# Attention of a hybrid block: six slots for a pair of heads instead of eight, and splits cut into a high and a low step

## The chip, the cores and the metric

The kernel runs on one core of a Trainium2 chip. The core has a matrix engine (PE), two element-wise engines (DVE, the vector engine, and ACT, the scalar engine, which alone computes exponentials), POOL (here: additions of a mask, and the issue of stores) and SP, which issues loads. Each engine takes its instructions in the order of its own queue and waits at the head of it for semaphores. The metric is the device time of one execution in microseconds.

## The reference

One layer of a streaming encoder on 1024 positions of width 1024. All of it is float32. The part that the change touches is the forgetting attention and the first half of the branch projection, which is computed beside it.

```python
def forgetting_attention(q, k, v, logf):
    c = jnp.cumsum(logf, axis=1).transpose(0, 2, 1)
    for s0 in range(0, s_len, Q_BLOCK):                   # query tiles of 128
        logits = einsum("bqhd,bkhd->bhqk", q[:, s0:s1], k[:, :s1]) * scale
        logits = logits + c[:, :, s0:s1, None] - c[:, :, None, :s1]
        logits = jnp.where(kpos <= qpos, logits, -jnp.inf)
        p = jax.nn.softmax(logits, axis=-1)
        outs.append(einsum("bhqk,bkhd->bqhd", p, v[:, :s1]))

ya = g_b * causal_depthwise_conv(g_c * hc, conv_w)
ya_d = jnp.einsum("bsc,cd->bsd", ya, w_branch[0])         # branch A, 512 -> 1024
yb_d = jnp.einsum("bsc,cd->bsd", yb, w_branch[1])         # branch B, of the attention
merged = jax.nn.sigmoid(gate_conv) * ya_d + jax.nn.sigmoid(gate_attn) * yb_d
```

There are 8 heads of 64 columns. Ahead of this stand the pre-norm and the input projection, behind it the output projection, two norms and a SwiGLU feed-forward layer.

## The kernel before

**Precision.** A float32 product is made of three passes over operands that are split in two: `hi`, a rounded copy that ACT writes, and `lo`, the remainder, a subtraction on DVE that needs `hi`. Each such split is thus one ACT instruction and one DVE instruction behind it (`split`, and for the queries and keys `split_q` and `split_k`).

**Pairs, rows, slots.** Heads are taken two at a time: pairs j = 0 to 3. The query tile i of a pair (a *row*, i = 0 to 7) needs keys up to its own tile, so it has i + 1 key blocks of 128. The list `steps` names a row for each slot: rows 7 down to 0 for pairs 0 to 2, and rows 3, 2, 1, 0, 7, 6, 5, 4 for pair 3; 32 slots in all. The work of a row passes through four stages, spread over three slots:

- slot t: PE writes the scores `sp` (three passes, both heads e = 0, 1 side by side in the array). A row of over 512 keys takes both of the two `S` buffers, one a head; a shorter row takes one buffer for both heads. DVE adds the bias `cb` and finds the row maximum in one instruction (`row_max`, writes `pt` and `nm`; in the queue listings below the two rows `ISA pt,nm<-sp,cb` and `ISA nm`). ACT takes the exponential in place (`expo`).
- slot t + 1: PE transposes `pt` by blocks into `tps`, at most 4 blocks to a bank, two banks (`turn_bank`). Each bank is drained to `ptT` by ACT or DVE. The drains are called `da`, `db` (head 0, blocks 0 to 3 and 4 to 7) and `dc`, `dd` (head 1).
- slot t + 2: PE multiplies `ptT` with the values into `po` (`pv_pair`). Behind a row with i a multiple of 4 ACT copies four finished rows to `yb`.

POOL adds the causal mask to the diagonal columns of `cb` just ahead of each row (`mask_of`).

**Fill.** Between the transposes of head 0 and those of head 1 PE does units of branch A (`pba`): one unit is three matmuls of 512 columns, four units make one output tile of 128 columns and half the positions, after which DVE multiplies it by a gate (`um`). 13 of the 16 tiles lie in the slots, 52 units; the table `units` says how many in which slot, from slot 8 on. The other three tiles follow after the last slot, and then branch B (`pbb`).

**The order is written out by hand.** From the last gate job to the end of the slots every instruction keeps its place in the program; nothing is moved by a scheduler. The table `at` lists what is appended to the end of a slot: loads (`load_pair`, `load_ya`, `load_wa`, `load_sg`, `load_wb`), splits (`split_q`, `split_k`, `split_ya`, `split_wa`, `split_wb`), the reciprocals of the row sums (`inverse`) and the divisions (`divide`). In a slot DVE sees: row maximum of head 0, `db`, row maximum of head 1, its share of `dc` and `dd`, the `um` products, and then the list of `at`. The slots 2 to 33 are the loop

```python
for t in range(2, NU + 2):
    ...
    for m in muls:
        m()
    for f in at.pop(t, ()):
        f()
```

Slots 0 and 1 (rows 7 and 6 of pair 0) are written into `last_pair`, between the products of the last gate job.

## Time and profile before

| | us |
|---|---|
| time, median of 3 runs | 1373.96 (1373.7 to 1374.09) |
| the profiled execution's own time | 1373.6 |
| its span on the core | 1371.8 |
| slots 2 to 33 and the three tiles behind them, first `sp` of slot 2 to first `pbb` | 422.26 to 582.48, 160.22 |
| pair 0's slots from 2 on / pair 1's eight / pair 2's eight / pair 3's eight, by their first `sp` | 21.88 / 43.44 / 40.25 / 37.39 |
| the rest, slots 32 and 33 and the three tiles | 17.26 |

Rows of the timeline read: start, duration, engine, line, operation, output and inputs, shape, count of like instructions merged into the row, and in brackets the idle time before it and what ended it. Almost every instruction has line 73, since a helper records them all, so tiles tell them apart. Matmuls are pipelined and their ends are modelled: a duration on PE overlaps the next instruction's, so what a piece of PE work costs is read from its start to the start of the next piece. Transposes and the products with the values work on plain float32; a value product counts as two matmul records.

### The profile page before, as it was taken

What the parts mean: (1) busy time and instruction counts of PE and PEld (TensorE: products, weight loads), DVE (VectorE), ACT (ScalarE), POOL (GpSimd) and SP (SyncE); (2) the same over time, 40 slices, a digit from 0 to 9 for tenths busy, and PEclk for the clock granted to TensorE, in tenths of its full rate; (3) what the DMA queues carried; (4) which work ended last, traced back from release to release, by engine and by line L of the source; (5) the groups of instructions that cost most, each with busy time, mean ns of one, the idle gap of its engine ahead of it and who ended that gap; (6) DMA issues with size and microseconds to landing.
All of it is one profiled execution on the core that took longest, in us unless ns stands there. A gap on an engine that the chain in (4) does not pass through costs nothing.

```text
span 1371.8 us, 17726 instructions
## 1 busy us (share of the span) xinstructions
PE 1341.8 (98%) x6725; PEld 1096.7 (80%) x6725; DVE 933.8 (68%) x1449; ACT 536.1 (39%) x853; POOL 127.9 (9%) x256
## 2 busy tenths in 40 slices
PE   7999999999999999999999999999999999999997
PEld 7978888888877777788887788888888888888886
DVE  6874767755446665685669698776677666676585
ACT  6641322233346654633447332232223223444452
POOL 0101000011112111000001112100111011000000
PEclk9999999999999999999999999999999999999999
DMA  6332423343315444462234565323333235975541
GB/s 216 97 111 85 137 57 99 94 123 100 114 71 185 135 131 152 139 215 85 77 124 153 158 201 179 100 73 110 108 107 105 95 115 205 352 251 197 168 162 62
DMA packets 153398, 186.88 MB, mean 136 GB/s; under 512 B 9424, under 2 KB 106768, under 8 KB 153312
## 3 DMA queue, kind: packets, MB, share of 16 engines
q1 hardware_dynamic: 138576, 137.19, 32.2%
q0 software_dynamic: 14736, 48.54, 9.7%
q8 instruction: 53, 0.87, 0.3%
q14 instruction: 33, 0.27, 0.1%
HBM read 136.62 MB, written 49.09 MB: 135 GB/s over the span
## 4 chain that ended last, share of the span: by engine, by line
PE 86%; DVE 5%; ACT 3%; DMA 3%; issue 2%; POOL 0%; DVEq 0%; ACTq 0%; POOLq 0%
PE b L73 52%; PE pd L73 15%; PE pm L73 5%; PE pbb L73 3%; PE pba L73 3%; PE po L73 2%; PE tps L73 2%; PE sp L73 2%; DVE t L73 1%; ACT pt L73 1%; DVE pt L73 1%; PE pv L73 1%; PE ma L73 1%; DMA pre_dram<-s 1%; PE tp L73 1%
## 5 line engine op out<-in xcount | busy, mean ns | idle before, releaser
L73 DVE TENSOR_TENSOR c<-c,b 128x512 f32<-128x512 f32 x195 | 133.2, 684 | 94.3 <-PE b L73 69.4
L73 DVE TENSOR_TENSOR lo<-raw,hi 128x1024 fp32r<-128x1024 f32 (+1 forms) x93 | 112.1, 1205 | 85.2 <-PE b L73 69.1
L73 ACT ACTIVATE hi<-raw 128x1024 fp32r<-128x1024 f32 (+1 forms) x100 | 101.8, 1018 | 130.6 <-PE b L73 81.1
L73 PE MATMUL b<-hth,hi 128*128 128x512 f32 x352 | 139.1, 395 | 0.5 <-DVE c L73 0.5
L73 PE MATMUL b<-hth,lo 128*128 128x512 f32 x352 | 138.1, 392 | 0.0
L73 PE MATMUL b<-htl,hi 128*128 128x512 f32 x352 | 137.2, 390 | 0.0
L73 ACT ACTIVATE hi<-sx 128x1024 fp32r<-128x1024 f32 x41 | 43.5, 1061 | 223.0 <-PE b L73 197.4
L73 PEld LDWEIGHTS b<-hth,lo 128*128 128x128 f32 x352 | 66.0, 188 | 15.6
L73 PEld LDWEIGHTS b<-hth,hi 128*128 128x128 f32 x352 | 66.1, 188 | 15.3 <-DVE c L73 1.5
L73 PEld LDWEIGHTS b<-htl,hi 128*128 128x128 f32 x352 | 66.1, 188 | 14.6
L73 DVE TENSOR_TENSOR lo<-sx,hi 128x1024 fp32r<-128x1024 f32 x41 | 50.2, 1225 | 34.4 <-PE b L73 30.8
L73 PE MATMUL b<-hah,hi 128*128 128x512 f32 x176 | 69.8, 399 | 1.0 <-ACT c L73 1.0
L73 DVE TENSOR_TENSOR sx<-raw 128x512 f32<-128x512 f32 x78 | 53.7, 689 | 22.9 <-DMA raw<-in_w_in_dram 11.0
L73 PE MATMUL b<-hah,lo 128*128 128x512 f32 x176 | 69.0, 393 | 0.0
L73 PE MATMUL b<-hal,hi 128*128 128x512 f32 x176 | 68.6, 390 | 0.0
L73 PE MATMUL pd<-hi,lo 128*128 128x512 f32 x160 | 62.6, 391 | 0.0
L73 PE MATMUL pd<-hi 128*128 128x512 f32 x160 | 62.3, 392 | 0.0
L73 PE MATMUL pd<-glo,ghi 128*128 128x512 f32 x148 | 57.7, 390 | 0.0
L73 PE MATMUL pd<-ghi 128*128 128x512 f32 x148 | 57.7, 390 | 0.0
L73 PE MATMUL pd<-ghi,glo 128*128 128x512 f32 x148 | 57.6, 389 | 0.0
L73 PE MATMUL b<-hT34h,lo 128*128 128x512 f32 x136 | 53.5, 394 | 0.0
L73 PE MATMUL b<-hT12h,lo 128*128 128x512 f32 x136 | 53.5, 394 | 0.0
(364 smaller groups left out, 3392.8 us busy)
## 6 DMA issues: line engine op xcount, KB each, us to landing
raw<-in_w_gate_up_dram SPq DMA_DIRECT2D x51, 512.0 KB, 4.0
raw<-in_w_in_dram SPq DMA_DIRECT2D x35, 512.0 KB, 4.2
a_dramS<-um POOLq DMA_DIRECT2D x44, 256.0 KB, 2.9
a_dramA<-um POOLq DMA_DIRECT2D x33, 256.0 KB, 2.9
xt<-in_x_dram SPq DMA_DIRECT2D x16, 512.0 KB, 3.9
sg<-sg_dram SPq DMA_DIRECT2D x32, 256.0 KB, 2.9
graw<-a_dramS SPq DMA_DIRECT2D x14, 512.0 KB, 7.9
sg_dram<-c POOLq DMA_DIRECT2D x24, 256.0 KB, 2.3
```

The source lines that it names most:

```text
L73: ins = getattr(self.engine, name)(*args, **kw)
```

## The change

Four things change, all in the slots.

1. **Six slots a pair.** Rows 3 and 2 share a slot, and rows 1 and 0. `steps` has 24 entries; pairs 0 to 2 run (7), (6), (5), (4), (3, 2), (1, 0), pair 3 runs (3, 2), (1, 0), (7), (6), (5), (4). The two rows of a shared slot lie one behind the other in one `pt` tile of each head (7 and 3 blocks), each has its own score buffer, and the slot's instructions run by `groups`: a slot with one row has the groups head 0, head 1; a shared slot has the groups first row (both heads), second row (both heads). The loop runs t = 2 to 25.
2. **Splits in two steps.** `split_q`, `split_k`, `split_ya`, `split_wa` and `split_wb` issue the ACT copy and return the DVE subtraction, which is called later. The table `cuts` names their slots. The copies are issued behind the first group's exponentials and ahead of `dc`; the subtractions (`lows`) at the end of the slot, ahead of the `um` products and of the list `at`.
3. **The fill is spread anew.** Again 13 tiles in 52 units, from slot 7 on, two to four units in most slots; the first four tiles run in the order (0, 0), (1, 0), (0, 1), (1, 1) (output tile, half). The value products come ahead of the reciprocal row's transpose `tr`.
4. **Loads.** `load_pair` becomes `k_load` and `q_load`. The biases, keys and values of pair 1 are issued before the loop, ahead of slot 2; those of pairs 2 and 3 in slots 7 and 13. The splits of the last two pieces of the branch B weights move from behind the loop into slots 24 and 25.

```diff
 def split_k(j, c):
     _, _, kh, kl = stacks[j]
     copy(kh[:, c], f32(kl[:, c]))
     if c.stop == S:
-        sub(kl, f32(kl), f32(kh))
+        return lambda: sub(kl, f32(kl), f32(kh))
...
-    steps = [(j, i) for j in range(3) for i in reversed(range(ST))]
-    steps += [(3, i) for i in (3, 2, 1, 0, 7, 6, 5, 4)]
+    steps = [(j, r) for j in range(3) for r in ((7,), (6,), (5,), (4,), (3, 2), (1, 0))]
+    steps += [(3, r) for r in ((3, 2), (1, 0), (7,), (6,), (5,), (4,))]
...
+    def halve(hi, lo, src):
+        copy(hi, src)
+        return lambda: sub(lo, src, f32(hi))
...
-    units = {}
-    for t in range(8, 32, 8):
-        if t < 24:
-            units |= {t: 1, t + 1: 1, t + 2: 1, t + 3: 1, t + 4: 2, t + 5: 2, t + 6: 4, t + 7: 4}
-        else:
-            units |= {t: 2, t + 1: 2, t + 2: 4, t + 3: 4, t + 4: 1, t + 5: 1, t + 6: 1, t + 7: 1}
-    units |= {32: 2, 33: 2}
+    units = {7: 2, 8: 2, 9: 4, 10: 4, 11: 4}
+    units |= {12: 3, 13: 1, 14: 2, 15: 2, 16: 4, 17: 4}
+    units |= {18: 2, 19: 2, 20: 3, 21: 1, 22: 2, 23: 2, 24: 4, 25: 4}
...
+    for j, k1_, k2_, q1_, q2_ in ((1, 2, 3, 4, 5), (2, 10, 10, 11, 11), (3, 14, 15, 16, 17)):
+        cuts[k1_] += [do(qk_tiles, j), do(split_k, j, n1)]
+        cuts[k2_].append(do(split_k, j, n2))
+        cuts[q1_].append(do(split_q, j, n1))
+        cuts[q2_].append(do(split_q, j, n2))
...
+    for d, t in enumerate((6, 8, 11, 13, 17, 20, 23, 25)):
+        cuts[t].append(do(split_wa, d))
+    for k, t in enumerate((20, 22, 24, 25)):
+        cuts[t].append(do(split_wb, k))
+    at[2].append(do(q_load, 1))
+    for t, j in ((7, 2), (13, 3)):
+        at[t] += [do(load_kv, j), do(q_load, j)]
...
+    load_kv(1)
     for t in range(2, NU + 2):
         turned = None
+        now = groups(t) if t < NU else ([], [])
         if t < NU:
             step_qk(t)
+        if t > 6:
+            pv_pair(t - 2)
         if t in rows:
             turned = inverse_rows(rows[t], pst, "mb")
...
-        if t < NU:
-            row_max(t, 0)
+        for i, e in now[0]:
+            row_max(t, i, e)
+        if t < NU and len(steps[t][1]) > 1:
+            mask_of(t, steps[t][1][1])
         if turned:
             turned()
         if back and db:
             db()
-        if t < NU:
-            expo(t, 0)
+        for i, e in now[0]:
+            expo(t, i, e)
+        lows = [f for f in (g() for g in cuts.pop(t, ())) if f]
         muls = [m for m in (next(fill, None) for _ in range(units.get(t, 0))) if m]
         if back:
             dc = turn_bank(back, 1, 0, "ACT" if wide else "DVE")
             dd = turn_bank(back, 1, 1, "DVE" if wide else "ACT")
-        if t < NU:
-            row_max(t, 1)
+        for i, e in now[1]:
+            row_max(t, i, e)
         if back:
             dc()
             if dd:
                 dd()
-        if t < NU:
-            expo(t, 1)
+        for i, e in now[1]:
+            expo(t, i, e)
         if t + 1 < NU:
-            mask_of(t + 1)
-        for m in muls:
-            m()
-        for f in at.pop(t, ()):
+            mask_of(t + 1, steps[t + 1][1][0])
+        for f in lows + muls + at.pop(t, []):
             f()
...
-    split_wb(2)
     for m in branch_a(KT - 1, 0, psm, "mm"):
         pass
...
-    split_wb(3)
```

What the tables make of the queues is seen at three places. The first is PE's queue at rows 3 and 2 of pair 0. Before, two slots:

```order
L73 MATMUL sp<-hi 128x512 x2
L73 MATMUL sp<-kl,hi 128x512 x2
L73 MATMUL sp<-hi,lo 128x512 x2
L73 MATMUL tps<-ident,pt 128x128 x5
L73 MATMUL po<-ptT,v_3314 64x128 x12
L73 MATMUL tps<-ident,pt 128x128 x5
L73 MATMUL sp<-hi 128x384 x2
L73 MATMUL sp<-kl,hi 128x384 x2
L73 MATMUL sp<-hi,lo 128x384 x2
L73 MATMUL tps<-ident,pt 128x128 x4
L73 MATMUL po<-ptT,v_3314 64x128 x10
L73 MATMUL tps<-ident,pt 128x128 x4
```

With the change, one slot:

```order
L73 MATMUL sp<-hi 128x512 x2
L73 MATMUL sp<-kl,hi 128x512 x2
L73 MATMUL sp<-hi,lo 128x512 x2
L73 MATMUL sp<-hi 128x384 x2
L73 MATMUL sp<-kl,hi 128x384 x2
L73 MATMUL sp<-hi,lo 128x384 x2
L73 MATMUL tps<-ident,pt 128x128 x5
L73 MATMUL po<-ptT,v_3314 64x128 x12
L73 MATMUL tps<-ident,pt 128x128 x5
```

The scores of row 2 stand directly behind those of row 3, and the transposes of both rows come together in the next slot, 7 blocks a head.

The second place is ACT's queue at the end of pair 0, where the queries of pair 1 are split (`hi<-raw`; the scores of pair 1's row 7 need them, and it is the first slot of that pair). Before:

```order
L73 ACTIVATE pt,rsum<-pt,nm 128x256 x2
L73 ACTIVATE hi<-lo 128x512
L73 ACTIVATE yh_3475<-raw 128x512
L73 ACTIVATE ptT<-tps 128x256
L73 ACTIVATE pt,rsum<-pt,nm 128x128 x2
L73 ACTIVATE yh_3475<-raw 128x512
L73 ACTIVATE s4h<-s_3684 128x512
L73 ACTIVATE ptT<-tps 128x128
L73 ACTIVATE pt,rsum<-pt,nm 128x1024 x2
```

With the change, slot 5, with rows 1 and 0, and the start of slot 6:

```order
L73 ACTIVATE ptT<-tps 128x512
L73 ACTIVATE yb<-po 128x512
L73 ACTIVATE pt,rsum<-pt,nm 128x256 x2
L73 ACTIVATE hi<-raw 128x512
L73 ACTIVATE ptT<-tps 128x512
L73 ACTIVATE pt,rsum<-pt,nm 128x128 x2
L73 ACTIVATE ptT<-tps 128x384
L73 ACTIVATE pt,rsum<-pt,nm 128x1024
```

The copies of a split stood at the end of a slot, behind all its exponentials; now they stand between the two groups. The second half of pair 1's queries is copied in the slot just ahead of row 7, behind a copy of `po` and two exponentials.

The third place is DVE's queue where pair 2 begins, from the row maxima of pair 1's row 0 to the first of pair 2's row 7. Before:

```order
L73 ISA pt,nm<-sp,cb 128x128
L73 ISA nm 128x1
L73 COPY ptT<-tps 128x256
L73 TENSOR_TENSOR um<-sg,pba 128x512
L73 TENSOR_TENSOR yb<-yb,rb 128x512
L73 TENSOR_TENSOR s4l<-s_4148,s4h 128x512
L73 ISA pt,nm<-sp,cb 128x1024
```

With the change:

```order
L73 ISA pt,nm<-sp,cb 128x128
L73 ISA nm 128x1
L73 COPY ptT<-tps 128x384
L73 SCALAR_TENSOR_TENSOR lo<-raw,hi 128x512 x2
L73 TENSOR_TENSOR s4l<-s_3998,s4h 128x512
L73 TENSOR_TENSOR um<-sg,pba 128x512
L73 TENSOR_TENSOR yb<-yb,rb 128x512
L73 ISA pt,nm<-sp,cb 128x1024
```

The two low halves of pair 2's queries, which stood in the slots of rows 3 and 2, now stand here, behind the drain that ends the slot, and the row maximum of row 7 stands behind five instructions instead of three.

## The prediction

> **What bounds the kernel now.** I began with the page's first part, then took the slots alone from the windows view, and then read PE's timeline there.

> ```profile
> span 1371.8 us, 17726 instructions
> PE 1341.8 (98%) x6725; PEld 1096.7 (80%) x6725; DVE 933.8 (68%) x1449; ACT 536.1 (39%) x853; POOL 127.9 (9%) x256
> ```

> PE is the bound. In the windows view of the slots (us, then busy time of PE, its weight loads, DVE, ACT, POOL, the clock, DMA) it is less clear:

> ```profile
> 422.26:582.48 160.22, 152.83 (x1309) 118.94 (x1309) 102.95 (x230) 96.72 (x216) 26.72 (x59) 1.00 0.48 155
> ```

> DVE is busy for 64% and ACT for 60% of these 160.22 us: no engine but PE is near its limit, and the clock is full. The row leaves PE 7.4 us of idle time. Since ends on PE are modelled I don't trust that figure and count the work by starts. The prices are starts to next starts in PE's timeline, at places where nothing waits:

> ```profile
> 431.61 0.49 PE L73 MATMUL sp<-hi 64*128 64x512 f32 x2
> 431.94 0.40 PE L73 MATMUL sp<-kl,hi 64*128 64x512 f32 x2
> 432.18 0.40 PE L73 MATMUL sp<-hi,lo 64*128 64x512 f32 x2
> 432.51 0.77 PE L73 MATMUL tps<-ident,pt 128*128 128x128 f32 x5
> ...
> 498.18 1.97 PE L73 MATMUL po<-ptT,v 128*64 128x128 f32 x32
> 500.07 0.98 PE L73 MATMUL tps<-ident,pt 128*128 128x128 f32 x7
> 500.81 0.48 PE L73 MATMUL pba<-yh,s4h 128*128 128x512 f32 x1
> 501.13 0.39 PE L73 MATMUL pba<-yl,s4h 128*128 128x512 f32 x1
> 501.36 0.40 PE L73 MATMUL pba<-yh,s4l 128*128 128x512 f32 x1
> 501.60 0.93 PE L73 MATMUL tps<-ident,pt 128*128 128x128 f32 x7
> 502.46 0.53 PE L73 MATMUL sp<-hi 64*128 64x320 f32 x2
> ```

> A value product costs 1.89/32 = 0.059, a transpose 0.74/7 = 0.106, a `pba` matmul 0.23 (501.13 to 501.36), a pair of `sp` matmuls of 512 keys 0.235 (0.24 in the row, less its rounding). The rest of these rows is what changing from one kind of work to another costs: 0.90 - 3 x 0.235 = 0.20 into `sp`, 0.79 - 0.69 = 0.10 into `pba`, 0.86 - 0.74 = 0.12 from `pba` to transposes. That is 0.42 a slot.

> The work in the 160.22 us is then: 36 key blocks in 4 pairs with 2 heads, two records each, 576 value products 34.0; 288 transposes less the 16 of slot 0's row 272, 28.8; 16 tiles of 12 `pba`, 192, 44.2; scores, 36 key blocks a pair at 3 x 0.235/4, 25.4 for four pairs, less 15 blocks of slots 0 and 1, 22.7; four `tr` 0.4. In all 130.1. So 30.1 us are lost in the slots, not 7.4: 32 x 0.42 = 13.4 in changes of work and **16.7 in stalls**.

> [...]

> ```profile
> 444.14 0.50 PE L73 MATMUL sp<-hi 64*128 64x512 f32 x1
> 445.89 0.50 PE L73 MATMUL sp<-hi 64*128 64x512 f32 x1 [1.25 <-DVE nm L73]
> ...
> 447.49 0.66 PE L73 MATMUL po<-ptT,v 128*64 128x128 f32 x8
> ...
> 492.25 0.47 PE L73 MATMUL sp<-hi 64*128 64x448 f32 x1 [0.68 <-DVE nm L73]
> ...
> 566.09 1.52 PE L73 MATMUL po<-ptT,v 128*64 128x128 f32 x22 [0.44 <-DVE ptT L73]
> ...
> 571.17 0.27 PE L73 MATMUL tr<-ident,ri 128*16 128x128 f32 x1 [0.92 <-ACT s4h L73]
> ```

> The scores of pair 1's row 7 take 3.35 us where 6 x 0.235 + 0.20 = 1.61 would do: 1.74 lost, of which 1.25 shows. PE waited for a score buffer, held by a row maximum that was late on DVE. Why DVE was late stands in the waits view (total us, times, longest):

> ```profile
> DVE yl L73 <- ACT yh L73: 6.9, 6, 1.7
> DVE lo L73 <- ACT hi L73: 6.3, 6, 1.6
> ```

> DVE stood 13.2 us at subtractions whose copy had not been made, with the next row's maximum behind them in its queue.

> **The change part by part.**

> *Fewer slots.* Every PE instruction of the slots stays. 24 slots instead of 32 change work 8 x 0.42 = 3.4 us less. In the 8 shared slots a second set of scores begins; no row before has one `sp` row behind another, so it costs 0 (the next pair of the same kind) to 0.20 (a change of work). I take 0.05, since the array's tiling stays: 0.4 in all. **-3.0**.

> *Stalls that go.* Rows 2, 1 and 0 had slots so short that drains and exponentials weren't done when PE came for them; in a shared slot they lie behind 4 to 7 us of PE work. The copies now stand ahead of `dc`, so subtractions find them made. The fill gives the wide rows more PE work. I let all 16.7 us go and put back what I find by walking each slot with these durations:

> - *Slot 6.* Its scores need the second query half, copied in slot 5 behind the copy of `po`, which waits for that slot's value products.

> ```profile
> 441.94 0.51 ACT L73 ACTIVATE pt<-pt,nm 128x256 f32<-128x256 f32 x1 [0.27 <-DVE nm L73]
> 442.36 0.19 ACT L73 ACTIVATION_READ_ACCUMULATOR pt<-pt,nm 128x1 f32 x1
> 442.45 0.49 ACT L73 ACTIVATE pt<-pt,nm 128x256 f32<-128x256 f32 x1
> 442.85 0.19 ACT L73 ACTIVATION_READ_ACCUMULATOR pt<-pt,nm 128x1 f32 x1
> 442.94 0.61 ACT L73 ACTIVATE hi<-lo 128x512 fp32r<-128x512 f32 x1
> 443.46 0.61 ACT L73 ACTIVATE yh<-raw 128x512 fp32r<-128x512 f32 x1
> ```

>    From the end of the value products: the copy of `po`, like any of 512 about 0.52 from start to start, two exponentials 0.51 + 0.49, the copy of the queries 0.61, and about 0.2 of signalling, 2.3. PE meanwhile has 7 transposes, 0.9. It stands 1.4, and 0.1 more for the low half: **1.5**. Behind that copy on ACT stand `dc` and row 0's exponentials, for which PE comes only after the scores. Row 7 of pair 1 lost 1.74 before, so this stall moves rather than goes.
> - *Slot 12.* Here the low halves are late:

> ```profile
> 474.50 0.69 DVE L73 SCALAR_TENSOR_TENSOR lo<-raw,hi 128x512 fp32r<-128x512 f32 x1 [1.00 <-ACT hi L73]
> 475.11 0.55 DVE L73 CUSTOM_DVE_ANT_0 pt<-sp,cb 128x384 f32<-128x384 f32 x1
> ...
> 482.78 0.56 DVE L73 COPY ptT<-tps 128x384 f32<-128x384 f32 x1 [2.90 <-PE tps L73]
> 483.26 0.68 DVE L73 TENSOR_TENSOR um<-sg,pba 128x512 f32<-128x512 f32 x1
> ```

>    From the last transpose: `dd` 0.48, two low halves 0.61 + 0.69, 1.8; PE can do the first four score matmuls, 0.6. **1.2**. Behind it three more DVE instructions of 0.6 delay row 7's maxima, but row 7's slot has 6 us of PE work, so that is covered; without the cover it would cost 1.8.
> - *Slots 24 and 25* have no scores ahead of the value products, so PE waits for the last drains as at 566.09 and 571.17: 0.44 and 0.92 are the rows' idle times, **1.4**.
> - *Second buffers and banks.* In slots 13 and 21 one unit is too little to cover `db` and the second row maximum, and in slots 9 to 11 the gap between a `um` product and the next use of its bank is under a microsecond. From 0 to 0.4 a slot, say **1.4**.
> - What I did not find: 24 slots at 0.1, **2.4**. From below nothing; from above half of what each slot lost before, 24 x 16.7/32/2 = 6.3.

> Stalls after: 7.9, so **-8.8**. The mask of a shared slot's second row now stands between its two groups:

> ```profile
> L73 POOL TENSOR_TENSOR cb<-cb,mask 128x128 f32<-128x128 f32 x62 | 28.0, 460 | 120.4 <-DVE nm L73 120.4
> ```

>    0.46 us a head, behind that head's row maximum; the other head's maximum and `db` cover it, and without them it would cost 8 x 0.46 = 3.7.

> *Loads* of pair 1 move ahead of slot 2, past the wait that held them:

> ```profile
> 424.57 0.81 SPq L73 DMA_DIRECT2D raw<-ya_dram  x2
> 425.43 0.91 SPq L73 DMA_DIRECT2D cb<-c_dram  x2
> ```

> They came right behind a load that waited for a free `raw` buffer. Nothing on PE waited for them, and they are needed earlier now (keys in slot 2): worth nothing by itself. The two weight splits that move into slots 24 and 25 shorten DVE's queue behind the slots, where 48 `pba` matmuls, 11 us, cover it either way: nothing.

> **The sum**: -3.0 - 8.8 = -11.8 us. The profiled execution took 1373.6, so 1361.8; the median is 0.36 higher, so **1362.2 us**. Behind the slots PE works without gaps, so the gain reaches the end.

> **The rivals.**

> *The slots get bound elsewhere.* In the shared slot (1, 0) of pairs 1 and 2 DVE has four short row maxima (each under the 0.55 of row 2 at 475.11), two drains of 0.48 and five instructions of 0.6 to 0.7, up to 6.3 us, against 6.4 on PE (20 value products, 14 transposes, 12 `pba`, scores and changes). If what is left over at its end isn't worked off, each shared slot loses about 0.8: 6.4 back, a gain of 5.4, **1368.6**. For it: the walk has margins under a microsecond in slots 9 to 13. Against: over all slots DVE's 102.95 us are 69% of 148.4.

> *The stalls only move.* If splitting in two steps and filling anew change nothing about the late row maxima, only the 3.0 go: **1371.0**, within what can be told from no change. For it: the subtractions still stand ahead of the next row's maximum. Against: the two waits rows, 13.2 us, which vanish by the order alone.

> *A copy waits for its load.* Copies now stand ahead of `dc` and of the second exponentials. One that waits for a DMA holds both, and then PE. The keys of pair 3 are issued when SP comes past a gate load that waits for slot 11's last `um` product, about 3 us into slot 12 (`dd`, two low halves, two more instructions), and copied in slot 14, about 10 us later (slots 12 and 13 have some 6 and 5 us of PE work).

> ```profile
> v<-v_dram SPq DMA_DIRECT2D x4, 512.0 KB, 10.3
> ...
> kl<-qk_dram SPq DMA_DIRECT2D x1, 512.0 KB, 9.3
> ```

> At 9.3 us from issue to landing there is hardly a margin; this decides from about 10 us on. [...] To end slower, over 11.8 us must come of it: four loads, keys and queries of pairs 2 and 3, each 4 us late, 16 us, **1378**. Against: pair 2's come three slots early, and the keys are the third of five loads, not the last.

> **How the numbers follow.** The forecast gets 0.72, the slots bound elsewhere 0.17, stalls that only move 0.07, late loads 0.04. The forecast's own bounds are 1359.4, with the last term and the second entries at nothing (-2.4 and -0.4), and 1367.3, with both at their upper ends (+3.9 and +1.2). To hold 8 in 10 the range goes a little over them, to **1359.0 to 1368.5**, nearly to the first rival. What a measurement can tell from no change is 0.2%, 2.7 us. Faster by more: 0.72 + 0.17 = 0.89, and half of the third at its edge, **0.91**; same **0.05**; slower **0.04**.

> **What would show it.** First `sp` of slot 2 to first `pbb` in about 148.4 us. The waits of DVE for `yh` and `hi` nearly gone. PE idle at the first scores of pair 1 (by ACT `hi`) and within those of pair 2 (by DVE `lo`), about 1.5 and 1.2, and no other gap over 1 us before slot 24. DVE's and ACT's busy times unchanged within 2 us. I am wrong if gaps on PE recur in each shared slot, if ACT's `hi` rows wait for DMA, or if the slots shrink and a later stage grows.

## The result, and the profile after

The changed kernel takes **1360.81 us**, the median of 4 runs (1360.34 to 1361.15), where the kernel before, beside it, took 1373.87. The ratio is 0.9905, with a 95% interval of 0.9887 to 0.9922: 13.1 us faster. The forecast was 1362.2, with a range from 1359.0 to 1368.5. The profiled execution took 1361.15 us.

The first line of the changed kernel's profile, and the windows view of its slots (first `sp` of slot 2 to first `pbb`):

```profile
span 1359.3 us, 17658 instructions
...
422.03:569.49 147.46, 143.76 (x1310) 117.48 (x1310) 101.74 (x225) 95.09 (x212) 26.75 (x59) 1.00 0.48 154
```

The slots went from 160.22 to 147.46 us, 12.76 less (148.4 had been forecast). They begin 0.23 us earlier, and what follows them takes 789.81 us, before 789.32, so 0.49 us more. That is the span's whole difference, 12.5 us. DVE and ACT did the same work (101.74 and 95.09 us, before 102.95 and 96.72).

PE's three largest waits in the slots of the changed kernel (total us, times, longest):

```profile
PE sp L73 <- ACT hi L73: 1.3, 1, 1.3
PE sp L73 <- DVE lo L73: 1.2, 1, 1.2
PE tr L73 <- DVE ri L73: 0.7, 1, 0.7
```

In PE's timeline I show the change from the first row's scores to the second's in slot 4, and then the places of the waits: the first scores of slot 6, those of slot 12, and the end of the slots.

```profile
431.92 0.40 PE L73 MATMUL sp<-hi,lo 64*128 64x512 f32 x2
432.15 0.34 PE L73 MATMUL sp<-hi 64*128 64x384 f32 x2
...
438.62 0.98 PE L73 MATMUL tps<-ident,pt 128*128 128x128 f32 x7
440.89 0.50 PE L73 MATMUL sp<-hi 64*128 64x512 f32 x2 [1.28 <-ACT hi L73]
...
479.71 0.50 PE L73 MATMUL sp<-hi,lo 64*128 64x512 f32 x2 [1.19 <-DVE lo L73]
...
555.45 0.43 PE L73 MATMUL po<-ptT,v 128*64 128x128 f32 x2
556.20 1.31 PE L73 MATMUL po<-ptT,v 128*64 128x128 f32 x18 [0.31 <-DVE ptT L73]
558.18 0.27 PE L73 MATMUL tr<-ident,ri 128*16 128x128 f32 x1 [0.68 <-DVE ri L73]
```

So there are two gaps of over 1 us, where the forecast had put them, and the two short ones of slots 24 and 25. The waits of DVE for `yh` are gone, and 0.9 us is left of those for `hi`. No copy on ACT waits for a load in the slots.

### The profile page after: what moved, and what is told of

Its sections match the earlier page's. It is cut to its first block, busy times and chain, and to the rows that moved or that the text cites. A ratio compares the mean times of both kernels' runs of the same rounds, so it can differ in the third digit from the quotient of the medians.

```text
span 1359.3 us, 17658 instructions
## 1 busy us (share of the span) xinstructions
PE 1332.5 (98%) x6725; PEld 1095.1 (81%) x6725; DVE 932.9 (69%) x1445; ACT 534.7 (39%) x849; POOL 127.6 (9%) x256
## 4 chain that ended last, share of the span: by engine, by line
PE 60%; DVE 2%; DMA 1%; ACT 1%; issue 0%; POOL 0%; DVEq 0%; ACTq 0%
PE b L73 29%; PE pd L73 16%; PE pm L73 5%; PE pbb L73 3%; PE pba L73 2%; PE po L73 1%; PE tps L73 1%; PE sp L73 1%; PE tp L73 0%; DVE tt L73 0%; DMA pre_dram<-c 0%; ACT tt L73 0%; DVE lo L73 0%; DMA raw<-in_w_gate_up_dram 0%; DMA pre_dram<-s 0%
## 5 line engine op out<-in xcount | busy, mean ns | idle before, releaser
L73 DVE TENSOR_TENSOR c<-c,b 128x512 f32<-128x512 f32 x195 | 133.3, 684 | 93.9 <-PE b L73 69.1
L73 DVE TENSOR_TENSOR lo<-raw,hi 128x1024 fp32r<-128x1024 f32 (+1 forms) x93 | 112.1, 1206 | 83.5 <-PE b L73 69.3
L73 ACT ACTIVATE hi<-raw 128x1024 fp32r<-128x1024 f32 (+1 forms) x100 | 101.7, 1018 | 131.1 <-PE b L73 76.9
L73 PE MATMUL b<-hth,hi 128*128 128x512 f32 x352 | 139.2, 395 | 0.0
L73 PE MATMUL b<-hth,lo 128*128 128x512 f32 x352 | 138.1, 392 | 0.0
L73 PE MATMUL b<-htl,hi 128*128 128x512 f32 x352 | 137.2, 390 | 0.0
L73 ACT ACTIVATE hi<-sx 128x1024 fp32r<-128x1024 f32 x41 | 43.5, 1061 | 222.7 <-PE b L73 197.0
L73 PEld LDWEIGHTS b<-hth,lo 128*128 128x128 f32 x352 | 66.0, 188 | 15.7
L73 PEld LDWEIGHTS b<-hth,hi 128*128 128x128 f32 x352 | 66.1, 188 | 14.7 <-DVE c L73 0.9
L73 PEld LDWEIGHTS b<-htl,hi 128*128 128x128 f32 x352 | 66.1, 188 | 14.6
L73 DVE TENSOR_TENSOR lo<-sx,hi 128x1024 fp32r<-128x1024 f32 x41 | 50.2, 1225 | 34.6 <-PE b L73 30.8
L73 PE MATMUL b<-hah,hi 128*128 128x512 f32 x176 | 69.8, 399 | 1.8 <-ACT c L73 1.8
L73 DVE TENSOR_TENSOR sx<-raw 128x512 f32<-128x512 f32 x78 | 53.7, 689 | 23.2 <-DMA raw<-in_w_in_dram 11.3
L73 PE MATMUL b<-hah,lo 128*128 128x512 f32 x176 | 69.0, 393 | 0.0
L73 PE MATMUL b<-hal,hi 128*128 128x512 f32 x176 | 68.6, 390 | 0.0
L73 PE MATMUL pd<-hi,lo 128*128 128x512 f32 x160 | 62.6, 391 | 0.0
L73 PE MATMUL pd<-hi 128*128 128x512 f32 x160 | 62.2, 392 | 0.0
L73 PE MATMUL pd<-glo,ghi 128*128 128x512 f32 x148 | 57.7, 390 | 0.0
L73 PE MATMUL pd<-ghi 128*128 128x512 f32 x148 | 57.7, 390 | 0.0
L73 PE MATMUL pd<-ghi,glo 128*128 128x512 f32 x148 | 57.6, 389 | 0.0
L73 PE MATMUL b<-hT34h,lo 128*128 128x512 f32 x136 | 53.5, 394 | 0.0
L73 PE MATMUL b<-hT12h,lo 128*128 128x512 f32 x136 | 53.5, 394 | 0.0
## 6 DMA issues: line engine op xcount, KB each, us to landing
raw<-in_w_gate_up_dram SPq DMA_DIRECT2D x51, 512.0 KB, 4.0
raw<-in_w_in_dram SPq DMA_DIRECT2D x35, 512.0 KB, 4.2
xt<-in_x_dram SPq DMA_DIRECT2D x16, 512.0 KB, 4.7
graw<-a_dramS SPq DMA_DIRECT2D x14, 512.0 KB, 3.7
```

Source lines behind the costliest of these rows:

```text
L73: ins = getattr(self.engine, name)(*args, **kw)
```

## Experiments

The forecast took the gain as one sum, so the first question is which edit brought it. Four kernels take the edits apart and two more check a reading of them; then come the stalls that are left, and the two rivals that had a price. All are read in two ways: by their ratio to the kernel before, and by the length of each pair on PE (from the first score matmul of its first slot to that of the next pair's; pair 0 from slot 2, pair 3 to the first `pbb`), in us:

| kernel | ratio (95%) | pair 0 | pair 1 | pair 2 | pair 3 | sum |
|---|---|---|---|---|---|---|
| before: eight slots, one step, old fill | 1 | 21.9 | 43.4 | 40.3 | 54.7 | 160.2 |
| eight slots, two steps, old fill | 1.0015 (1.0006 to 1.0024) | 21.4 | 43.1 | 41.6 | 54.8 | 161.0 |
| eight slots, two steps, new fill in pairs 2 and 3 | 0.9980 (0.9971 to 0.9988) | 21.4 | 43.1 | 38.7 | 54.4 | 157.6 |
| six slots, one step, new fill | 1.0006 (0.9998 to 1.0015) | 21.0 | 45.1 | 38.4 | 56.8 | 161.2 |
| the same, queries cut a slot earlier | 0.9975 (0.9966 to 0.9984) | 19.5 | 42.9 | 38.6 | 57.4 | 158.4 |
| after: six slots, two steps, new fill | 0.9905 (0.9887 to 0.9922) | 18.9 | 36.9 | 38.0 | 53.7 | 147.5 |

**Two steps alone, in the kernel before.**

```diff
-        at[t].append(do(split_ya, n, m))        # and so for q, k, wa, wb
+        cuts[t].append(do(split_ya, n, m))
...
             expo(t, 0)
+        lows = [f for f in (g() for g in cuts.pop(t, ())) if f]
...
-        for m in muls:
-            m()
-        for f in at.pop(t, ()):
+        for f in lows + muls + at.pop(t, []):
             f()
```

> The kernel before, eight slots a pair, fill and loads and slot numbers of all splits as before, but each split in two steps: the copy on ACT behind the first exponential, the subtraction at the slot's end. Theory: the 13.2 us that DVE stood at copies go, and with them most of the 7.7 us that the wide rows lost: 1374 - 5 = 1369 (1367 to 1371); the short rows keep their losses (3.5 us) and the 32 slots their 13.4 us of changes. Rival (two rows in one slot did it all): 1373 to 1374, because the copies now delay the drain and the second exponential by as much as they spare DVE.

Measured: 1375.6 us beside 1373.6, a little slower. The waits for copies did go. These are DVE's waits for them, and PE's four longest sums, in the slots of this kernel:

```profile
DVE yl L73 <- ACT yh L73: 1.1, 2, 0.6
DVE lo L73 <- ACT hi L73: 0.7, 2, 0.5
```

```profile
PE sp L73 <- DVE nm L73: 2.1, 4, 0.7
PE tr L73 <- DVE um L73: 1.7, 2, 1.5
PE pba L73 <- DVE um L73: 1.6, 2, 1.1
PE tr L73 <- DVE ri L73: 1.6, 1, 1.6
```

In the kernel before, PE had of these:

```profile
PE sp L73 <- DVE nm L73: 3.3, 5, 1.2
...
PE tr L73 <- DVE um L73: 0.5, 2, 0.3
```

The 13.2 us at copies became 1.8, and DVE's waits for transposes grew by 13.6 (from 32.0 to 45.6): most of what DVE did not stand at copies any more it waited for PE. PE's waits for row maxima fell from 3.3 to 2.1 us, but those for products and reciprocals rose from 0.5 to 4.9. The reason lies in the same edit: the subtractions now stand on DVE ahead of the `um` products and the reciprocals, behind which they stood before. The slot of pair 2's row 0 in this kernel, DVE and then PE:

```profile
522.51 1.22 DVE L73 TENSOR_TENSOR lo<-lo,hi 128x1024 fp32r<-128x1024 f32 x1
...
524.24 0.68 DVE L73 TENSOR_TENSOR um<-sg,pba 128x512 f32<-128x512 f32 x1
...
524.98 0.51 PE L73 MATMUL pba<-yh,s4h 128*128 128x512 f32 x1 [1.10 <-DVE um L73]
```

The same place in the kernel before, where PE does not wait:

```profile
523.51 0.68 DVE L73 TENSOR_TENSOR um<-sg,pba 128x512 f32<-128x512 f32 x1
...
524.71 1.22 DVE L73 TENSOR_TENSOR lo<-lo,hi 128x1024 fp32r<-128x1024 f32 x1
```

By the starts, slots 6 to 10, 29 and 30 are 2.5 us shorter than before, and slots 12, 15, 23 and the end from slot 31 on are 3.2 us longer, each with such a wait. So the two steps did free PE in part, and the new order took it back; with eight slots, two steps and the `um` products ahead of the subtractions nothing was run. My theory falls here, also because row 6's scores in pair 2 wait 0.68 us as they did before. The rival's time is nearly met (1373 to 1374), but not its reason, and the next kernel shows that merging rows did not do it all.

**Six slots and the new fill, splits in one step.**

```diff
-        lows = [f for f in (g() for g in cuts.pop(t, ())) if f]
...
-        for f in lows + muls + at.pop(t, []):
+        for g in cuts.pop(t, ()):
+            low = g()
+            if low:
+                low()
+        for f in muls + at.pop(t, []):
```

> The changed kernel, six slots a pair, fill and loads as changed, but each split in one step: copy and subtraction both at the slot's end, where the low halves stood. Theory (the gain of 8.8 us came mostly from DVE no longer standing at subtractions whose copy is not made): the rows DVE yl <- ACT yh and DVE lo <- ACT hi come back, one wait of about 1 us for each of some 15 split places, the next row's maximum is late behind them, and the wide rows lose what they lost before, by the starts 1.7 + 2.4 + 0.8 + 1.4 + 1.4 = 7.7 us. Part of that is covered by the new fill: 1361 + 5 = 1366 (1364 to 1369). Rival (two rows in one slot did it all, since the short rows were what lost time): the waits come back on DVE but PE does not see them, 1361 to 1362.

Measured: 1374.8 us beside 1373.6. Both miss, mine by 9 us: without the two steps, six slots and the new fill bring nothing at all, with the splits in the change's slots and in its order, ahead of the `um` products and the reciprocals. (Before, they stood behind these, and four of the eight `ya` splits stood in pair 0's slots; six slots with that were not run.) PE's waits in the slots of this kernel:

```profile
PE sp L73 <- ACT hi L73: 4.2, 2, 2.2
PE pba L73 <- DVE um L73: 3.2, 5, 1.5
PE tr L73 <- DVE ri L73: 2.6, 2, 1.5
```

Pair 1, whose six slots hold all eight splits of `ya`, is 8.2 us longer than in the changed kernel, and pair 2 only 0.3. Some 1.7 of the 8.2 are PE's clock (0.53 over 3.60 us), told in the last section. Two things came together in this edit: the copies come at the slot's end, and DVE stands at them. The next two kernels part them.

**The same, with the query halves cut a slot earlier.**

```diff
-    for j, k1_, k2_, q1_, q2_ in ((1, 2, 3, 4, 5), (2, 10, 10, 11, 11), (3, 14, 15, 16, 17)):
+    for j, k1_, k2_, q1_, q2_ in ((1, 2, 3, 4, 4), (2, 10, 10, 10, 10), (3, 14, 15, 16, 16)):
```

> The kernel with splits in one step at the slot's end (1374.8), with the query halves cut one slot earlier, so that a slot lies between their copy and their first use. Theory A (what the one step costs is mostly that a copy at the end of a slot is too late for the next slot's scores): the 4.2 us at sp <- ACT hi go and what was late behind them, 1374.8 - 6 = 1369 (1367 to 1371). Theory B (it is mostly DVE standing 20 us at copies, with row maxima, products and drains behind it): 1374.8 - 4.2 + some standing in the earlier slots = 1372 to 1374.

Measured: 1371.2 us beside 1374.7, between the ranges of A and B; by the slots 2.8 us less than with one step, where the query wait alone had been 4.2. The row `sp <- ACT hi` is gone, and 158.4 us are still 10.9 more than the changed kernel's. So late query copies are the smaller part, and most of the loss is of B's kind: PE has no wait for a copy left, and its rows for `um` and `ri`, which on DVE stand behind the subtractions that wait, are still there, with 4.5 and 2.6 us of 9.1 in all. Some 1.7 us more are the clock, at about half for some 3.4 us in pair 3: by the starts a `pba` matmul there takes 0.43 us (568.20 to 568.63), where 0.23 is the price.

```profile
PE pba L73 <- DVE um L73: 4.5, 3, 2.7
PE tr L73 <- DVE ri L73: 2.6, 2, 1.5
```

**Copies where the change has them, each subtraction right behind its copy.**

```diff
-        lows = [f for f in (g() for g in cuts.pop(t, ())) if f]
+        for g in cuts.pop(t, ()):
+            low = g()
+            if low:
+                low()
```

> The changed kernel with the copies where it has them, behind the first exponentials, but each subtraction right behind its copy, ahead of the other row maxima and the drains on DVE. This parts the two things that the one step brought together. Theory A (DVE standing at copies is what costs): DVE stands 1 to 2 us at each of some 15 places, 20 us in all, and PE loses as with one step less the 4 us of late query halves, 1368 to 1372. Theory B (the place of the copies at the slot's end is what costs, DVE standing is idle time that it would spend elsewhere): 1360 to 1363.

Measured: 1389.4 us beside 1374.3, ratio 1.0113 (1.0097 to 1.0128). A's direction, and 17 us beyond its range. PE's first wait in this kernel, then DVE's largest at copies:

```profile
PE sp L73 <- DVE nm L73: 16.4, 14, 2.6
```

```profile
DVE lo L73 <- ACT hi L73: 14.8, 10, 3.6
```

A subtraction that stands ahead of the second row maxima holds the score buffers, and the next scores on PE wait for them, 14 times. So this kernel prices the place of the subtraction, and not the standing alone. Neither half of the two steps is enough: with copy and subtraction both at the slot's end the time was 1374.8, with both early it is 1389.4, and only the copy early and the subtraction behind row maxima and drains gives 1360.8. Some 10 us of the excess are the clock (0.94 over the slots), told in the last section.

**The new fill as well, in eight slots with two steps.**

```diff
-            units |= {t: 1, t + 1: 1, t + 2: 1, t + 3: 1, t + 4: 2, t + 5: 2, t + 6: 4, t + 7: 4}
...
-            units |= {t: 2, t + 1: 2, t + 2: 4, t + 3: 4, t + 4: 1, t + 5: 1, t + 6: 1, t + 7: 1}
-    units |= {32: 2, 33: 2}
+    units = {8: 1, 9: 1, 10: 1, 11: 1, 12: 2, 13: 2, 14: 4, 15: 4}
+    units |= {16: 3, 17: 1, 18: 2, 19: 2, 20: 2, 21: 2, 22: 2, 23: 2}
+    units |= {24: 1, 25: 1, 26: 1, 27: 1, 28: 3, 29: 1, 30: 2, 31: 2, 32: 4, 33: 4}
```

> Eight slots a pair and the loads as before, splits in two steps, and now also the fill of pairs 2 and 3 moved from the short rows to the wide ones as in the change (8 of 16 units in rows 7 to 4 where 4 stood). Theory (each loss of the wide rows had two causes, subtractions waiting for copies and too little PE work between one row's scores and the next, and only both edits together free PE): the 1.1 to 1.3 us lost at row 6's scores of pair 2 and around row 7 and 6 of pair 3 go, 1375.6 - 4 = 1371.6 (1370 to 1373). Rival (without two short rows in one slot nothing goes, since the fill taken from the short rows uncovers as much there): 1375 to 1377.

Measured: 1380.0 us beside 1374.7, ratio 1.0044 (1.0031 to 1.0056), slower still. But pair 2 fell from 41.6 to 38.7 us, as the theory has it, while pair 3 grew from 54.8 to 61.9, for a reason of its own. ACT's row in pair 3:

```profile
ACT s4h L73 <- PE pba L73: 6.8, 2, 4.7
```

With the fill stretched out, a weight buffer was still held when its next copy came, and the copy stood on ACT ahead of the drain. PE's mean granted clock over the profiled execution was 0.996 too, where the changed kernel's was 0.999: over 1376.8 us some 4 us, by estimate; how much of that lies in pair 3 was not shown. So a second kernel moves the last weights too:

```diff
-    for d, t in enumerate((4, 8, 12, 15, 19, 23, 26, 29)):
+    for d, t in enumerate((4, 8, 12, 15, 19, 23, 26, 30)):
         at[t].append(do(load_wa, d))
-    for d, t in enumerate((4, 8, 14, 16, 22, 24, 27, 32)):
+    for d, t in enumerate((4, 8, 14, 16, 22, 24, 30, 32)):
         at[t].append(do(load_sg, d))
-    for d, t in enumerate((7, 11, 15, 18, 22, 25, 28, 32)):
+    for d, t in enumerate((7, 11, 15, 18, 22, 25, 30, 33)):
```

> Eight slots, splits in two steps, fill of pairs 2 and 3 moved to the wide rows, and now the last branch weights loaded and split one or two slots later too, so that their copies on ACT need not wait 4.7 us for the buffer that a pba unit holds (that wait put 7 us into pair 3 in the run before, while pair 2 went from 41.6 to 38.7 us). Theory (fill and two steps work together on wide rows also in eight slots): pair 2 stays near 38.7, pair 3 with its drains comes to 52 to 54 instead of 54.8, 1375.6 - 2.9 - 2 = 1370.7 (1369.5 to 1372.5); what is then left to the changed kernel, some 10 us, is what two short rows in one slot bring. Rival (pair 3 loses by itself what pair 2 gains): 1374 to 1377.

Measured: 1371.1 us beside 1374.3, within the theory's range: pair 2 again 38.7, pair 3 54.4 (52 to 54 expected). Row 6's scores in pair 2, which had waited 0.68 us for a score buffer before, come without a wait behind three units of fill:

```profile
491.05 0.27 PE L73 MATMUL tps<-ident,pt 128*128 128x128 f32 x1
491.25 0.50 PE L73 MATMUL sp<-hi 64*128 64x448 f32 x2
```

From here to the changed kernel (157.6 to 147.5) 10.1 us remain: 2.5 in pair 0, 6.2 in pair 1, 0.6 and 0.7 in pairs 2 and 3. Pair 1's part holds merging, fill and the slots of the `ya` splits together, since with eight slots these were left as before. The new fill with splits in one step was not run in eight slots.

**Less fill behind rows 7 and 6, in the changed kernel.**

```diff
-    units |= {12: 3, 13: 1, 14: 2, 15: 2, 16: 4, 17: 4}
-    units |= {18: 2, 19: 2, 20: 3, 21: 1, 22: 2, 23: 2, 24: 4, 25: 4}
+    units |= {12: 0, 13: 0, 14: 4, 15: 4, 16: 4, 17: 4}
+    units |= {18: 4, 19: 4, 20: 0, 21: 0, 22: 2, 23: 2, 24: 4, 25: 4}
```

> The changed kernel with less fill behind wide rows, nearer to the spread of before: pair 2 has none in the slots of rows 7 and 6 and four units in each later slot, pair 3 four in each shared slot and none in those of rows 7 and 6. Theory (fill behind the wide rows is one of the causes that must be there): row 6's scores in slots 13 and 21 wait about 1.2 us each for row 7's maxima, and the slots behind lose some more, 1361 + 4 = 1365 (1363 to 1367). Rival (two rows in a slot already put enough PE work there): 1360.5 to 1362.

Measured: 1363.7 us beside 1374.7, ratio 0.9921 (0.9909 to 0.9934), in the theory's range; the slots take 150.70 us, 3.2 more. Part of the loss is where it was looked for: by the starts row 6's scores take 1.88 us in pair 2 and 2.41 in pair 3, where they took 1.42 in the changed kernel, so 0.5 and 1.0 more (1.2 each expected). The other 1.7 us are not located in full; a wait of 0.70 us behind row 6 of pair 3 is among them:

```profile
535.38 0.44 PE L73 MATMUL sp<-hi 64*128 64x448 f32 x1 [0.55 <-DVE nm L73]
...
539.38 1.43 PE L73 MATMUL tps<-ident,pt 128*128 128x128 f32 x8 [0.70 <-ACT ptT L73]
```

**The two query stalls.** In slot 5 the copy goes ahead of the copy of `po`, and in slots 5, 11 and 17 the subtractions go ahead of the last drain.

```diff
             da()
+        lows = None
+        if t == 5:
+            lows = [f for f in (g() for g in cuts.pop(t, ())) if f]
         if t <= 6:
             pv_pair(t - 2)
...
             row_max(t, i, e)
+        if t in (5, 11, 17):
+            for f in lows:
+                f()
+            lows = []
         if back:
             dc()
```

> The changed kernel with two orders altered: in slot 5 the copy of the second query half goes on ACT ahead of the copy of the value products, and in slots 5, 11 and 17 the subtractions go on DVE ahead of the last drain. Theory (two stalls left at the first scores of pairs 1 and 2, 1.4 and 1.4 us by the starts, are due to these halves being late in their queues, and nothing else is late right behind): the idle rows at sp (1.3 by ACT hi, 1.2 by DVE lo) vanish, 1360.8 - 2.8 = 1358.0 (1357.6 to 1358.8). Rival (PE would only wait at the next thing, the exponentials of the row pair, so the stalls move): 1360 to 1361, with idle rows at tps <- ACT pt in slots 6 and 12.

Measured: **1357.2 us** beside 1373.6, ratio 0.9879 (0.9866 to 0.9893); the slots take 144.5 us, 3.0 less. That is 0.4 us under the theory's range. Both gaps are gone and nothing took their place; the first scores of slots 6 and 12 come without idle time:

```profile
439.50 0.50 PE L73 MATMUL sp<-hi 64*128 64x512 f32 x2
...
476.24 0.49 PE L73 MATMUL sp<-hi 64*128 64x512 f32 x2
```

**The end of the slots**, first with all the fill of slots 24 and 25 ahead of their value products, and the last reciprocal ahead of the subtractions:

```diff
+        if t >= NU:
+            muls = [m for m in (next(fill, None) for _ in range(units.get(t, 0))) if m]
         if t > 6:
             pv_pair(t - 2)
```

> The changed kernel, but in slots 24 and 25, which have no scores, the fill is issued on PE ahead of the value products, and the reciprocal of the last row sums ahead of the subtractions. Theory (PE waits there only because the last drains lie right ahead of it: by the starts 0.54 and 1.42 us): both go, 1360.8 - 1.9 = 1358.9 (1358.7 to 1359.6). Rival (the drains behind the slots are what the next stage waits for, so PE waits at pbb instead): 1360.5 to 1361.

Measured: 1367.8 us beside 1373.6, ratio 0.9959 (0.9947 to 0.9972), 7 us slower than the changed kernel (by the slots of the profiled execution 5.0), which neither theory had. PE's first wait:

```profile
PE pba L73 <- DVE um L73: 4.2, 2, 2.5
```

There is one bank for the fill. Its next unit waits until the last product has been read, and the value products had been the cover for that. The second form keeps one unit of a tile back to open the next slot, with its product right behind, on top of the query orders:

```diff
+        first = next(fill) if t >= NU else None
+        if first:
+            first()
         if t > 6:
             pv_pair(t - 2)
...
-    units |= {18: 2, 19: 2, 20: 3, 21: 1, 22: 2, 23: 2, 24: 4, 25: 4}
+    units |= {18: 2, 19: 2, 20: 3, 21: 1, 22: 2, 23: 1, 24: 3, 25: 4}
```

> The kernel with both query orders altered (1357.2), and at the end of the slots one unit of fill kept back: slots 23 and 24 issue one unit less, and slots 24 and 25 begin with it, ahead of their value products, with its product right behind, so that the bank is free again when the next unit comes; the last reciprocal goes ahead of the subtractions. Theory (what made the fill ahead of the value products slow was only the wait of the next unit for its bank, 4.2 us at pba <- DVE um, which a finished unit does not have): the 2.0 us of slots 24 and 25 go, 1357.2 - 1.9 = 1355.3 (1355.0 to 1356.2). Rival (the bank again): 1357 or above, with idle rows at pba <- DVE um.

Measured: **1356.4 us** beside 1374.7, ratio 0.9871 (0.9857 to 0.9884), the lowest ratio of all, though its interval overlaps that of the kernel without this. It is just above the theory's range (1355.0 to 1356.2) and below the rival's 1357. Its slots and their end:

```profile
422.25:565.26 143.01, 142.65 (x1310) 117.31 (x1309) 101.61 (x225) 94.84 (x212) 27.16 (x59) 1.00 0.50 159
```

```profile
554.00 0.50 PE L73 MATMUL pba<-yh,s4h 128*128 128x512 f32 x1 [0.31 <-DVE um L73]
```

The slots take 1.5 us less than without it, not 1.9. Two more changes of work, by the price of the forecast 0.4, and a wait of 0.31 us account for what is missing; the changes were not measured alone.

**A late load, and more work on DVE.** The loads of pair 2 two slots later, and each `um` product of the shared slots done twice:

```diff
-    for t, j in ((7, 2), (13, 3)):
+    for t, j in ((9, 2), (13, 3)):
```

```diff
+        if t < NU and len(steps[t][1]) > 1:
+            muls = muls + muls
```

> The changed kernel with the loads of pair 2 issued at the end of slot 9 instead of slot 7, so that the keys are asked for some 6 us ahead of their copy in slot 10 instead of 19 us. Issue to landing took 9 to 10 us, so the copy should wait about 4 us with the drain and the second exponentials behind it on ACT. Theory (the rival of late loads, priced at about 4 us each): an idle row at ACT hi <- DMA of about 4 us, PE idle behind it by 3 to 4, 1364 to 1365. Rival (PE has other work): 1361 to 1362.

> The changed kernel with each um product of the shared slots done twice on DVE (five more instructions of 0.6 us, in slots 10, 11, 16, 17 and 19; the second writes the same values again). Theory (the shared slots are not bound by DVE: over all slots it is busy 69%): at most 1 us more, 1361 to 1362. Rival (the shared slots are at DVE's limit, the first rival of the forecast): 3 us more, 1364.

The late load: 1362.7 us, ratio 0.9918 (0.9904 to 0.9931); the slots take 149.63 us, 2.2 more, all of it in pair 1 (39.1 us instead of 36.9). The time lies between the theory's range and the rival's. ACT's row and what PE saw of it:

```profile
ACT hi L73 <- DMA kl<-qk_dram: 3.2, 1, 3.2
```

```profile
474.79 0.43 PE L73 MATMUL po<-ptT,v 128*64 128x128 f32 x2 [1.15 <-ACT ptT L73]
```

The mechanism is real: the drain stood behind the copy that waited, and value products behind the drain. Its price is two thirds of the lateness.

The doubled products: 1362.7 us, ratio 0.9919 (0.9905 to 0.9932), not told apart from the changed kernel. The median lies between the theory (1361 to 1362) and the rival (1364). By its profile the slots take 0.9 us more for five products, 3.4 us of DVE work:

```profile
422.20:570.57 148.37, 144.26 (x1309) 117.51 (x1309) 105.38 (x231) 95.50 (x212) 26.71 (x59) 1.00 0.48 153
```

So the shared slots have some room left on DVE, though not all of it is free. The profiled execution is the fastest of the five, with 1360.9 us, so by the time alone the rival is not excluded.

## Why the prediction was right, and where not

Its time and its list of stalls held; its reason for the largest term held only in part.

- *What bounds the slots.* 130.1 us of work and 0.42 us a slot for changes are borne out. In the last kernel of the study with the fill kept back, which has hardly a wait left, 143.01 - 130.1 - 24 x 0.42 = 2.8 us remain. By the starts 0.5 of these are the last `tr` with the wait behind it, 0.4 its two changes more, and 0.6 the scores of row 5 in pairs 2 and 3, 1.53 us each where 1.25 would do.
- *Fewer slots, -3.4, and second entries, +0.4.* The last pair of score matmuls of row 3 takes 0.23 us to the first of row 2 (431.92 to 432.15), its price without any change of work: the entry costs nothing. That the array's tiling is the reason (64*128 in both rows) was my estimate; no run varies it alone. The changes themselves were not measured alone.
- *Stalls left, 7.9.* By the same count 147.46 - 130.1 - 10.1 = 7.3 were left. Slot 6: 1.5 forecast, 1.65 by the starts (1.40 ahead of the first scores and 0.25 within them). No row gives the 0.2 for signalling in its sum; in the changed kernel ACT's copy of the queries ends at 440.84 and PE's first score starts at 440.89, 0.05 later. Slot 12: 1.2 forecast, 1.4. Slots 24 and 25: 1.4 forecast, 2.0; here I had taken the idle times of the rows before, and by the starts they are longer. The mis-sized terms are the unseen ones, second buffers and what I did not find: 3.8 forecast, 2.2 measured. They came 1.6 under, the named stalls 0.9 over and the entries 0.4 under: about the 0.9 us between 148.4 and 147.46.
- *The step that failed* is the reason given for "stalls that go": that DVE was late because it "stood 13.2 us at subtractions whose copy had not been made". Take that standing away in eight slots, and PE's waits for row maxima fall only from 3.3 to 2.1 us. Row 6's wait in pair 2 stays at 0.68 us and goes with the new fill. What is won is lost again at products and reciprocals behind the subtractions (4.9 us of waits where 0.5 were). What the runs show in its place is that the edits depend on each other and on the order on DVE. New fill with two steps takes 2.9 us out of pair 2, with eight slots. Six slots with the new fill and one step gain nothing: there DVE's standing and the late copies do reach PE, by the 10.0 us of waits for `hi`, `um` and `ri`. In the orders run here, the two steps are worth -0.8 us in eight slots and 13.7 in six, of which some 1.7 are the clock. What six slots bring without the new fill stays open.
- *The mask, the loads, the weight splits.* In the slots of the changed kernel the waits view has for PE, DVE and ACT no wait for a mask or for a load of pairs 1 to 3 (POOL waits 4.3 us for two loads of `cb`), and the 48 `pba` matmuls behind the slots take 11.28 us for 11.0 of work.
- *The slots bound elsewhere* (1368.6): against it, no gaps that recur in the shared slots of the changed kernel, and 0.9 us by the slots for the doubled products. *Stalls only move* (1371.0): false for the change as a whole, true for two steps in eight slots, which I had not thought of as apart: there the stalls moved from row maxima to products and reciprocals. *A copy waits for its load* (1378): it did not happen. One load 3.2 us late cost 2.2, so four loads 4 us late would be some 11 us by that row, not 16. The way there is the rival's: PE waited for a drain that only stood behind the copy.

## What to carry to other kernels

An idle row on an engine that is not the bound tells what it waited for, not that the wait costs anything: take it away alone and see whether the bound engine moves (here 13.2 us of waits became 1.8, and the time went from 1373.6 to 1375.6). Then read the bound engine's waits by cause, since a total that stays can hide one wait that went and another that came: here the edit that took the waits away also put other work ahead of the products that PE waits for. When several edits go together, their worth can't be split in advance; here splitting in two steps was worth nothing in one schedule and 13.7 us in the next. In a queue worked off in order, put the first half of a two-engine job early, and the second behind everything that the bound engine waits for: here 1360.8 us, with both late 1374.8, with both early 1389.4.

## What the hardware showed that was not expected

In some kernels a gap on PE cost more than its length, because PE's clock fell behind it. In the kernel with six slots and one step, by the windows view (the last figures of a row are clock, DMA share and GB/s):

```profile
440.95:442.94 1.99, 0.00 (x2) 0.01 (x2) 0.58 (x2) 1.93 (x8) 0.35 (x1) 1.00 0.00 0
442.94:446.54 3.60, 3.60 (x16) 2.22 (x16) 1.26 (x2) 0.00 (x0) 0.00 (x0) 0.53 0.40 136
```

and by its timeline:

```profile
442.94 0.75 PE L73 MATMUL sp<-hi 64*128 64x512 f32 x2 [1.99 <-ACT hi L73]
443.48 0.63 PE L73 MATMUL sp<-lo,hi 64*128 64x512 f32 x2
443.91 0.64 PE L73 MATMUL sp<-hi,lo 64*128 64x512 f32 x2
...
488.02 0.50 PE L73 MATMUL sp<-hi 64*128 64x512 f32 x2 [2.16 <-ACT hi L73]
488.35 0.39 PE L73 MATMUL sp<-kl,hi 64*128 64x512 f32 x2
```

Behind the gap of 1.99 us a pair of score matmuls takes 0.43 us instead of 0.235, for 3.6 us, and 0.47 x 3.6 = 1.7 us are lost beside the gap itself. Behind a longer gap of 2.16 us the clock stays full.

In the kernel with the subtractions right behind their copies, the clock over all its slots is 0.94:

```profile
423.46:601.00 177.54, 157.93 (x1316) 126.88 (x1314) 104.16 (x227) 97.22 (x212) 27.00 (x60) 0.94 0.40 128
```

That is 0.06 x 177.5, some 10 of the 29.4 us by which its slots (176.9 us from first `sp` to first `pbb`) are longer than the changed kernel's. Half is what the rows show. One gap of 1.99 us had it behind it and one of 2.16 us did not, so the length of a gap alone does not tell.

The traces show a little more. In steps of 2 us the kernel with the subtractions right behind their copies reads:

```profile
440.00:442.00 2.00, 1.45 (x11) 1.35 (x12) 1.78 (x9) 1.31 (x4) 1.40 (x4) 0.73 0.00 0
442.00:444.00 2.00, 2.00 (x16) 1.67 (x16) 0.56 (x1) 0.60 (x1) 1.21 (x3) 0.50 0.00 0
444.00:446.00 2.00, 1.74 (x19) 1.33 (x15) 0.00 (x0) 1.13 (x4) 0.00 (x0) 0.91 0.00 0
446.00:448.00 2.00, 0.49 (x1) 0.18 (x1) 1.00 (x4) 1.51 (x5) 0.00 (x0) 0.94 0.00 0
448.00:450.00 2.00, 1.84 (x8) 1.50 (x10) 0.58 (x3) 0.81 (x4) 0.00 (x0) 0.50 0.57 175
450.00:452.00 2.00, 2.00 (x10) 0.98 (x8) 1.20 (x2) 0.04 (x1) 0.00 (x0) 0.50 0.23 87
452.00:454.00 2.00, 2.00 (x20) 2.00 (x22) 0.04 (x2) 2.00 (x5) 0.45 (x1) 0.50 0.00 0
454.00:456.00 2.00, 1.79 (x16) 1.16 (x12) 1.88 (x4) 1.13 (x3) 0.00 (x0) 0.85 0.01 4
...
458.00:460.00 2.00, 2.00 (x15) 1.42 (x13) 1.04 (x2) 0.50 (x2) 0.00 (x0) 0.50 0.86 292
460.00:462.00 2.00, 2.00 (x17) 1.67 (x14) 0.06 (x2) 0.88 (x2) 0.45 (x1) 0.65 0.49 147
...
474.00:476.00 2.00, 1.56 (x13) 1.23 (x15) 1.81 (x6) 1.03 (x2) 0.46 (x1) 0.77 0.48 139
476.00:478.00 2.00, 2.00 (x20) 2.00 (x22) 0.64 (x2) 0.00 (x0) 0.45 (x1) 0.50 0.00 0
478.00:480.00 2.00, 2.00 (x21) 1.77 (x18) 0.52 (x2) 0.40 (x1) 0.00 (x0) 0.88 0.00 0
...
560.00:562.00 2.00, 2.00 (x17) 1.46 (x16) 0.85 (x1) 0.70 (x2) 0.00 (x0) 0.60 0.99 369
562.00:564.00 2.00, 2.00 (x15) 1.67 (x12) 0.25 (x2) 0.65 (x2) 0.45 (x1) 0.55 0.08 33
```

```profile
439.61:443.02 3.41, 1.10 (x9) 0.63 (x8) 1.86 (x9) 3.27 (x11) 1.69 (x4) 1.00 0.00 0
443.02:446.43 3.41, 3.41 (x15) 2.14 (x15) 1.07 (x2) 0.00 (x0) 0.00 (x0) 0.50 0.41 138
...
483.98:487.39 3.41, 1.88 (x12) 1.39 (x10) 0.56 (x1) 1.82 (x7) 0.14 (x1) 1.00 0.01 2
487.39:490.80 3.41, 2.70 (x28) 1.83 (x30) 3.32 (x6) 1.09 (x3) 0.00 (x0) 1.00 0.03 8
```

The gap of 1.99 us lies whole in one piece of the grid, with 2.31 us idle in all; the gap of 2.16 is divided, with 1.53 us idle in one piece and 0.71 in the next. In the slots of these three kernels, each cut by its own grid, the three pieces at full clock with the most idle PE (1.8, 2.3 and 2.5 us by the timelines) were followed by half clock, and none with less than 1.4; with 1.4 to 1.7 both occurred. So in these runs the idle time in one piece of the grid fits where the length of a gap does not. What decides between 1.4 and 1.7 stays open.
